# HGRN2 steps that make their own weight pairs on ScalarE and VectorE, in a two-layer encoder trunk

## The chip, the core and the metric

The kernel runs on one core of one Trainium2 chip. The metric is the device time of one execution in microseconds (us). Five engines work side by side, each with its own queue that runs in order: TensorE (PE; its weight loads are PEld), VectorE (DVE), ScalarE (ACT), GpSimd (POOL) and SyncE (SP, which here only issues transfers).

## The reference, cut to what matters

Layer 0 is a sparse attention beside a gMLP gate, layer 1 is an HGRN2 recurrence; each is followed by a ConvFFN. D = 1024, T = 1024, f32.

```python
def hgrn2(q, f, i, lb):                      # 8 heads, chunks of 64
    q = silu(q); g = lb + (1 - lb) * sigmoid(f)
    k = 1.0 - g; log_g = log(g)
    def step(S, (qb, kb, ib, lgb)):
        b = cumsum(lgb, axis=-2)
        inter = (qb * exp(b)) @ S
        a = einsum('td,tsd,sd->ts', qb, where(causal, exp(b_t - b_s), 0), kb)
        S_new = exp(b_last)[..., None] * S + (kb * exp(b_last - b)).T @ ib
        return S_new, inter + a @ ib
...
# layer 1: q, f, i, gate = split_cols(h @ c_w_in); o = rms_norm(hgrn2(...), c_out_norm)
#          y = (o * silu(gate)) @ c_w_out
# layer 0: dsa_attention: top-256 keys of an indexer's score per query, then softmax(q k + bias) v over those
```

## The kernel before, in words

Every large product is taken with a high and a low f32r part of both operands: three matmuls (lines 107 to 109, `mm3`). So each block of weights (128x1024 f32, tile `raw`, two buffers) is turned into a pair `whi`, `wlo` (four buffers each). `weights` does it on POOL: a copy that rounds (line 76) and a subtraction (line 77). `split` (lines 111 to 113) does the same on ACT and DVE; it serves activations.

The attention of layer 0 (pools `at`, `at2`) runs 48 steps: eight heads, six steps each over the query blocks (0,1), (2,3), 4, 5, 6, 7. At step t PE makes the logits of step t (`probabilities`), turns the probabilities of step t-2 (`transposed`), and for odd heads multiplies the values of step t-3 (`values`, line 595) for that head and the even one before it. So the values of a pair of heads lie in six steps in a row, and the next six have none. PE's order is the written one here (`manual_schedule`); the other engines are ordered by a planner from its own costs. Before it stand the top-256 search on DVE (lines 492 to 528) and the projections; `v_t` takes its last columns by four ACT copies (line 477).

The HGRN2 layer is 64 steps: eight groups (two halves of the sequence by four pairs of heads), and in each group eight steps p = 0 to 7, four chunks of 128 for two heads. PE, DVE and ACT keep the written order in the whole loop; POOL and SP follow the planner. A step s, in order of writing:

- `exponents` of step s+2: four matmuls into `ep`, two ACT exponentials (line 870) into `ex`; `operands` of s+2: nine DVE instructions (lines 879 to 887).
- a piece of the next group's projections, one of two kinds by p: `forget`, `query`, `value`, or this group's `gate`. Its 24 or 48 matmuls (lines 107 to 109) are most of PE's step. `forget` ends in a sigmoid and three DVE instructions (lines 824 to 826: gates and key).
- `output` of step s: three products into `ok`, a tile of `bank` (two buffers), where `at` is an operand (line 968); ACT copies the result, DVE updates the state from it (line 975).
- `levels` of step s+1: products into `lv` (line 939), and from them `at`: a DVE product with the identity (944), three DVE masked copies, three ACT block copies (951), two more DVE masked copies (954).

Once per group and half of it: `logs` (Ln, its high part on ACT, its low part `ll` on POOL, line 832) at p = 2; `key_turn` at the end of p = 3, 4 (with two POOL products for `gq`, lines 846 and 847); and for the group before: `squares` and `sums` at p = 0, 1, `spread` (two diagonal tiles `dg` on DVE, line 913) at p = 3, 4, `broadcast` (PE, line 919, into a tile of `bank`) at the start of p = 4, 5 and `finish` (DVE, 923 and 924) after it. In the last group p = 2 to 7 hold `out_chunk`, columns of the output projection of the first half.

Of the kernel before, what the change touches and what calls it, by code (L numbers as in the profile page):

```python
# [38 lines left out]
def trunk(ctx, tc, a, out):  # L39
# [29 lines left out]
    def weights(src, place, m=1024, on_pool=True):  # L69
# [10 lines left out]
        return hi, lo  # L80

# [325 lines left out]
    with pool_("gm2", 2) as gp2, pool_("gm", 1) as gp, pool_("bis", 2) as bp, pool_("up", 1) as up_:  # L407
# [135 lines left out]
    with tc.tile_pool(name="at", bufs=1, reuse_waits="tile") as ap1, tc.tile_pool(name="at2", bufs=2, reuse_waits="tile") as ap2:  # L543
# [30 lines left out]
        def transposed(hd, i, l):  # L574
# [23 lines left out]

        ops, yo = ops + (bias_of(0, ap1),), None
        steps = [(hd, ii) for hd in range(8) for ii in ((0, 1), (2, 3), (4,), (5,), (6,), (7,))]  # L600
        ls, pts = {}, {}
        with tc.manual_schedule(engines={mybir.EngineType.PE}):
            for t in range(len(steps) + 3):
# [9 lines left out]
                if 2 <= t < len(steps) + 2:  # L613
                    hd, ii = steps[t - 2]
                    for i in ii:
                        pts[hd, i] = transposed(hd, i, ls.pop((hd, i)))
                if t >= 3 and steps[t - 3][0] % 2:
                    hd, ii = steps[t - 3]
                    for i in ii:
# [3 lines left out]
                        if i % 4 == 3:  # L623
                            split(y[i // 4][0][:, hd // 2], y[i // 4][1][:, hd // 2], yo)
    mix0.close()
# [151 lines left out]
    class Group:  # L777


        def __init__(self, hf, hp):  # L780
            self.hf, self.hp = hf, hp
            self.qs, self.gs, self.kT, self.gq, self.kh, self.oS, self.sq2 = ([None, None] for _ in range(7))
            self.wt = {}

        def silu(self, c0, e, nm, bufs, o=None):

            wt = w_cols(wc, c0 + (2 * self.hp + e) * P)
# [15 lines left out]
        def wide(self, c0, n, o):  # L803

            if n == 0:
                self.wt[c0] = w_wide(wc, c0 + 256 * self.hp)
            for d in range(2):
                tmaj(o[:, 256 * d:256 * d + 256], self.wt[c0], h, 4 * self.hf + 2 * n + d)
            return o.rearrange("p (c n) -> p c n", c=2)

        def forget(self, n, o=None):
# [8 lines left out]
            bc = lambda r: self.lb[:, r:r + 1].to_broadcast([P, 2, 256])  # L820
            g, k = self.i_t[:, 2 * n:2 * n + 2], self.k_t[:, 2 * n:2 * n + 2]
            o = self.wide(1024, n, pbank()) if o is None else o.rearrange("p (c n) -> p c n", c=2)
# [15 lines left out]
        def key_turn(self, e):  # L838
# [91 lines left out]
    def levels(G, c, e, ex, kl, dl, q_, k_):  # L930
        at = hw.tile([P, P], FT, name="at")
        for n in (1, 0):
            lv = lv_pool.tile([P, H], FT, name="lv")
            if n:
                pe.matmul(lv[:, 3 * P:], k_, q_, start=True, stop=True)
            for l in range(4 * n, 7 if n else 4):
# [8 lines left out]
            for l in range(4 * n, 7 if n else 4):  # L945
                w, ls = LEVELS[l], slice((l - 4 * n) * P, (l - 4 * n) * P + P)
                v = lv[:, ls]
                if l < 2:

                    for b in range(0, P, 2 * w):  # L950
                        act.copy(at[b:b + w, b + w:b + 2 * w], v[b:b + w, b + w:b + 2 * w])
                else:
                    v = second(v, w) if w > 1 else v[:, 0:64].rearrange("p (b w) -> p b w", w=w)
                    dve.copy_predicated(second(at, w), lmask[:, 64 * l:64 * l + 64].rearrange("p (b w) -> p b w", w=w), v)
        return G, c, e, ex, dl, at

    def output(G, c, e, ex, dl, at):
# [19 lines left out]
    def out_chunk(m):  # L977

        wt = w_cols(a["c_w_out"][0], m * P)
# [14 lines left out]
    steps = [(g, c, e) for g in groups for c in range(4) for e in range(2)]  # L994
    G = groups[0]
    for n in range(2):
        G.forget(n, fg[n])
    G.logs()
    for n in range(2):

        G.value(n, lv_pool.tile([P, H], FT, name="lv"))
    G.query(0, ex_pool.tile([P, H], FT, name="ep"))
    with tc.manual_schedule(engines={mybir.EngineType.PE, mybir.EngineType.DVE, mybir.EngineType.Activation}):
        G.key_turn(0)
        G.key_end(0)
        ops = [G.operands(*G.exponents(0, 0)[1:])]
        G.query(1, pbank())
        G.key_turn(1)
        ats = [levels(*ops.pop(0))]
        ops.append(G.operands(*G.exponents(0, 1)[1:]))  # L1010
        for s, (G, c, e) in enumerate(steps):
# [5 lines left out]
            if g in (4, 5, 7) and p in (2, 5, 6, 7) and not (g == 5 and p > 5):  # L1017
                back = (G if g == 7 else groups[3]).fetch((2, 5, 6, 7).index(p) + (4 if g == 5 else 0))
            if p == 0:
                G.key_end(1)  # L1020
            if p in (4, 5) and L:
                L.broadcast()
            if p == 6 and N:
                N.key_end(0)
# [152 lines left out]
```

## Time and profile before

| | us |
|---|---|
| three timed runs | 2982.4, 2980.08, 2980.15 (median 2980.15) |
| profiled execution | 2982.33, of which the span from first to last instruction is 2980.5 |
| PE busy | 2835.9 (95% of the span) |
| DVE / ACT / POOL busy | 1912.8 / 867.2 / 1254.8 |
| granted PE clock, mean over the span | 0.981 |

The profile gives each instruction's start and length on its engine, and for an idle engine the instruction that ended its wait. The sequence of stages by time: projections and search to 473 us, attention to about 613, output projection and first ConvFFN to about 1465, HGRN2 to about 2190, then the second output projection and ConvFFN.

### The profile page before, as it was taken

How to read it: one execution, taken by the hardware profiler on the slowest of the kernel's cores; microseconds unless marked ns; L12 is line 12 of the kernel's file. 1: busy time of each engine (PE TensorE's matmuls, PEld its weight loads, DVE VectorE, ACT ScalarE, POOL GpSimd, SP SyncE). 2: the span in 40 equal slices, each digit the busy share in tenths (PEclk: the TensorE clock that was granted, in tenths of full speed). 3: DMA queues.
4: the chain of work that ended last, by engine and by line, in shares of the span. 5: the costliest groups of instructions: out<-in, count | busy, mean ns of one | idle time of the engine just before them, and what ended most of it. 6: DMA issues, size and time to landing. Idle time of an engine off the chain costs nothing.

```text
span 2980.5 us, 39089 instructions
## 1 busy us (share of the span) xinstructions
PE 2835.9 (95%) x15173; PEld 2403.8 (81%) x15188; DVE 1912.8 (64%) x3739; ACT 867.2 (29%) x1644; POOL 1254.8 (42%) x820
## 2 busy tenths in 40 slices
PE   7989996999999999999889999999999999999998
PEld 6779885778888888888788898888778888888887
DVE  5779998746545544545877777877665544445446
ACT  4555314622111111112343333333222111111112
POOL 3116622366433433334554444444355433434433
PEclk9999998999999999999899999999999999999999
DMA  4301222333111111112322212222252111111112
GB/s 164 94 29 40 85 85 57 86 110 117 43 57 50 50 44 49 50 43 76 105 63 64 65 54 67 65 71 68 85 166 71 50 43 43 57 50 44 49 50 78
DMA packets 243524, 204.09 MB, mean 68 GB/s; under 512 B 9137, under 2 KB 215778, under 8 KB 243338
## 3 DMA queue, kind: packets, MB, share of 16 engines
q1 hardware_dynamic: 230704, 177.68, 19.2%
q10 hardware_dynamic: 12634, 23.90, 2.6%
q8 instruction: 120, 1.97, 0.3%
q14 instruction: 66, 0.54, 0.1%
HBM read 180.01 MB, written 26.26 MB: 69 GB/s over the span
## 4 chain that ended last, share of the span: by engine, by line
PE 73%; DVE 19%; ACT 4%; POOL 2%; issue 1%; DMA 0%; ACTq 0%; POOLq 0%; SPq 0%; DVEq 0%
PE pbank L107 10%; PE pbank L108 10%; PE pbank L109 10%; DVE junk L492 6%; PE dn L107 5%; PE dn L108 5%; PE dn L109 5%; PE bank L107 5%; PE bank L109 5%; PE bank L108 5%; PE lv L939 2%; DVE cand L512 1%; DVE ex L882 1%; PE pbank L595 1%; PE twobank L363 1%
## 5 line engine op out<-in xcount | busy, mean ns | idle before, releaser
L76 POOL TENSOR_SCALAR whi<-raw 128x1024 fp32r<-128x1024 f32 x268 | 289.7, 1084 | 915.0 <-PE pbank L108 503.3
L77 POOL TENSOR_TENSOR wlo<-raw,whi 128x1024 fp32r<-128x1024 f32 x268 | 652.4, 2438 | 17.8
L107 PE MATMUL pbank<-bhi,whi 128*128 128x512 f32 (+2 forms) x1352 | 522.6, 387 | 3.3 <-DVE xt L638 3.0
L108 PE MATMUL pbank<-blo,whi 128*128 128x512 f32 (+2 forms) x1352 | 522.9, 387 | 0.0
L109 PE MATMUL pbank<-bhi,wlo 128*128 128x512 f32 (+2 forms) x1352 | 522.2, 386 | 0.0
L687 DVE TENSOR_TENSOR xt<-xt,dn 128x512 f32<-128x512 f32 x352 | 235.0, 682 | 151.5 <-PE dn L109 151.2
L654 DVE SCALAR_TENSOR_TENSOR cy<-pbank,col_cv,cy 128x511 f32<-128x511 f32 (+1 forms) x176 | 130.8, 743 | 293.7 <-ACT cy L653 293.7
L107 PEld LDWEIGHTS pbank<-bhi,whi 128*128 128x128 f32 (+1 forms) x1352 | 255.1, 189 | 55.1 <-POOL whi L76 3.8
L109 PEld LDWEIGHTS pbank<-bhi,wlo 128*128 128x128 f32 (+1 forms) x1352 | 255.1, 189 | 52.1
L108 PEld LDWEIGHTS pbank<-blo,whi 128*128 128x128 f32 (+1 forms) x1352 | 255.3, 189 | 50.3
L654 DVE SCALAR_TENSOR_TENSOR cy<-bank,col_cv,cy 128x511 f32<-128x511 f32 (+1 forms) x176 | 131.8, 749 | 241.6 <-ACT cy L653 238.7
L107 PE MATMUL dn<-ghi,whi 128*128 128x512 f32 x704 | 279.1, 397 | 0.6 <-ACT ghi L675 0.5
L108 PE MATMUL dn<-glo,whi 128*128 128x512 f32 x704 | 279.0, 396 | 0.0
L109 PE MATMUL dn<-ghi,wlo 128*128 128x512 f32 x704 | 278.5, 396 | 0.0
L107 PE MATMUL bank<-bhi,whi 128*128 128x512 f32 x704 | 274.8, 390 | 0.0
L109 PE MATMUL bank<-bhi,wlo 128*128 128x512 f32 x704 | 274.1, 389 | 0.0
L108 PE MATMUL bank<-blo,whi 128*128 128x512 f32 x704 | 273.9, 389 | 0.0
L676 POOL TENSOR_TENSOR glo<-cy,ghi 128x512 fp32r<-128x512 f32 x88 | 114.3, 1298 | 344.7 <-ACT ghi L675 344.7
L653 ACT ACTIVATE cy<-bank,col_cv,col_cv 128x512 f32<-128x512 f32 x88 | 68.1, 774 | 473.9 <-PE bank L109 473.9
L492 DVE TENSOR_SCALAR_CACHE_REDUCE junk<-tri,cand 128x1024 bf16<-128x1024 f32 (+1 forms) x186 | 175.9, 946 | 0.0
L654 DVE SCALAR_TENSOR_TENSOR cy<-halo,col_cv,cy 128x1 f32<-128x1 f32 (+1 forms) x176 | 173.8, 987 | 0.0
L107 PEld LDWEIGHTS dn<-ghi,whi 128*128 128x128 f32 x704 | 132.3, 188 | 33.4 <-DVE xt L687 1.0
(325 smaller groups left out, 5821.7 us busy)
## 6 DMA issues: line engine op xcount, KB each, us to landing
raw<-in_ffn_w_up_dram SPq DMA_DIRECT2D x96, 512.0 KB
raw<-in_c_w_in_dram SPq DMA_DIRECT2D x64, 512.0 KB
raw<-in_ffn_w_down_dram SPq DMA_DIRECT2D x48, 512.0 KB
raw<-in_ab_w_in_dram SPq DMA_DIRECT2D x28, 512.0 KB
raw<-in_ab_w_out_dram SPq DMA_DIRECT2D x16, 512.0 KB
raw<-in_c_w_out_dram SPq DMA_DIRECT2D x16, 512.0 KB
xo<-xd ACTq DMA_DIRECT2D x24, 256.0 KB
ts_d<-td ACTq DMA_DIRECT2D x8, 576.0 KB
```

The source lines that it names most:

```text
L76: pool.tensor_scalar(out=hi, in0=raw, scalar1=1.0, scalar2=1.0, op0=OP.mult, op1=OP.mult)
L77: pool.tensor_tensor(out=lo, in0=raw, in1=f(hi), op=OP.subtract)
L107: pe.matmul(o, lhs[0], rhs[0], start=start, stop=False)
L108: pe.matmul(o, lhs[0], rhs[1], start=False, stop=False)
L109: pe.matmul(o, lhs[1], rhs[0], start=False, stop=stop)
L363: pe.matmul(s[:, c0:c0 + cn], q_, ka[:, c0:c0 + cn], start=True, stop=False)
L492: dve.tensor_scalar(out=junk[:, 0:n], in0=acc[i], scalar1=cand, scalar2=None, op0=OP.is_ge, op1=OP.add, accum_out=cnt)
L653: act.activation(y, o, AF.Identity, scale=cw2[:, c:c + 1], bias=cb[:, c:c + 1])
L654: mac = lambda d, s_, w: dve.scalar_tensor_tensor(out=d, in0=s_, scalar=w[:, c:c + 1], in1=d, op0=OP.mult, op1=OP.add)
L676: pool.tensor_tensor(out=lo, in0=yb, in1=f(hi), op=OP.subtract)
L687: dve.tensor_tensor(out=xt[hf][:, m], in0=xt[hf][:, m], in1=o, op=OP.add)
L939: pe.matmul(lv[:, ls], kl[:, l], ex[:, l], start=True, stop=True)
```

## The change

In HGRN2, `raw_unit` loads the weights of one unit one step ahead; `pair_of` splits them on ACT and DVE, one unit in each of the 64 steps (`ahead` says which), one step or more before PE uses it; the first two units of group 1 are split ahead of the loop. POOL makes no pair for the groups 1 to 7 and for `out_chunk`. The low part of the logarithm and `gq` go from POOL to DVE, and the key 1 - g from DVE to ACT. The masks of `at` are made in two parts: the fine levels as before, the ACT blocks and the last two masked copies at the start of the next step. Gates, logs, key turn, spread, broadcast, finish and key end each come a step later or in smaller pieces. In the attention the values of the first three pairs of heads lie in every second step of eleven; all values stand ahead of the transposes of their step, `pt1` has nine buffers, and the instructions that the attention puts on the engine of `v_last` are queued behind it.

```diff
+    def raw_unit(src, place):
+
+        raw = wpool.tile([P, 1024], FT, name="raw", bufs=2)
+        nc.sync.dma_start(place(raw), src)
+
+        def pair_of():
+            hi, lo = (wpool.tile([P, 1024], FR, name=n, bufs=4) for n in ("whi", "wlo"))
+            split(hi, lo, raw)
+            return place(hi), place(lo)
+
+        return pair_of
...
-                act.activation(v_t[:, 4 * hf:4 * hf + 4, 256 * c:256 * c + 256], o, AF.Copy)
+                v_last = act.activation(v_t[:, 4 * hf:4 * hf + 4, 256 * c:256 * c + 256], o, AF.Copy)
...
-    with tc.tile_pool(name="at", bufs=1, reuse_waits="tile") as ap1, tc.tile_pool(name="at2", bufs=2, reuse_waits="tile") as ap2:
+    with tc.tile_pool(name="at", bufs=1, reuse_waits="tile") as ap1, tc.tile_pool(name="at2", bufs=2, reuse_waits="tile") as ap2, \
+            tc.issue_after(v_last.ins):
...
-                pt = ap2.tile([P, H], FT, name="pt1", bufs=6) if hd % 2 else all_[:, g * P:g * P + w]
+                pt = ap2.tile([P, H], FT, name="pt1", bufs=9) if hd % 2 else all_[:, g * P:g * P + w]
...
+        for t, (hd, ii) in enumerate(steps):
+            if hd % 2:
+                when[t + 3 + (t % 6 if hd < 7 else 0)] = (hd, ii)
...
-                if t >= 3 and steps[t - 3][0] % 2:
-                    hd, ii = steps[t - 3]
+                if t in when:
+                    hd, ii = when[t]
...
-            act.activation(g, o, AF.Sigmoid)
+            self.f[n] = self.wide(1024, n, pbank()) if o is None else o.rearrange("p (c n) -> p c n", c=2)
+
+        def sigmoids(self):
+
+            for n in range(2):
+                act.activation(self.i_t[:, 2 * n:2 * n + 2], self.f[n], AF.Sigmoid)
+
+        def gates(self):
+            bc = lambda r: self.lb[:, r:r + 1].to_broadcast([P, 4, 256])
+            g = self.i_t
             dve.tensor_tensor(out=g, in0=g, in1=bc(1), op=OP.mult)
             dve.tensor_tensor(out=g, in0=g, in1=bc(0), op=OP.add)
-            dve.tensor_scalar(out=k, in0=g, scalar1=-1.0, scalar2=1.0, op0=OP.mult, op1=OP.add)
 
         def logs(self):
             g = self.i_t
+            act.activation(self.k_t, g, AF.Identity, scale=-1.0, bias=ones[:, 0:1])
             act.activation(g, g, AF.Ln)
             act.activation(self.lh, g, AF.Copy)
-            pool.tensor_tensor(out=self.ll, in0=g, in1=f(self.lh), op=OP.subtract)
+
+        def low_logs(self):
+            dve.tensor_tensor(out=self.ll, in0=self.i_t, in1=f(self.lh), op=OP.subtract)
...
+        def odd_queries(self, e):
+
             q, t = self.qs[e], hw.tile([P, 256], FT, name=f"gq{e}")
-            pool.tensor_tensor(out=t, in0=odd(q), in1=odd(self.kT[e]), op=OP.mult)
-            pool.tensor_tensor(out=t, in0=odd(q), in1=t, op=OP.subtract)
+            dve.tensor_tensor(out=t, in0=odd(q), in1=odd(self.kT[e]), op=OP.mult)
+            dve.tensor_tensor(out=t, in0=odd(q), in1=t, op=OP.subtract)
...
-        wt = w_cols(a["c_w_out"][0], m * P)
+        wt = groups[7].pairs.pop(0)
...
                 x = n[0].exponents(*n[1:])
-                ops.append(n[0].operands(*x[1:]))
+
+            at, low = ats[0][-2:]
+            blocks(at, low)
+            if x:
+                ops.append(x[0].operands(*x[1:]))
+            for l in (2, 3):
+                masked(at, low, l)
+            to, pair_of = made
+            to.pairs.append(pair_of())
+            made = ahead(s + 1) if s + 1 < len(steps) else None
+            if p in (5, 6) and L:
+                L.finish(p - 5)
             if p in (4, 5) and L:
-                L.finish(p - 4)
-            if p in (3, 4) and L:
-                L.spread(p - 3)
+                L.spread(p - 4)
...
             if N:
+                if p == 2:
+                    N.gates()
+                if p == 3:
+                    N.logs()
+                if p == 4:
+                    N.low_logs()
+                if p in (5, 6):
+                    N.odd_queries(p - 5)
                 (N.forget, N.query, N.value, G.gate)[p // 2](p % 2)
+                if p == 1:
+                    N.sigmoids()
```

## Rows read from the trace of the kernel before

**Rows 1.** The page, its first part: busy us of each engine.
```profile
PE 2835.9 (95%) x15173; PEld 2403.8 (81%) x15188; DVE 1912.8 (64%) x3739; ACT 867.2 (29%) x1644; POOL 1254.8 (42%) x820
```
**Rows 2.** Busy time in stretches: ConvFFN; then HGRN2's eight groups and their sum.
```profile
core 0: us, PE busy (x) PEld busy (x) DVE busy (x) ACT busy (x) POOL busy (x), PEclk, DMA share, GB/s
...
760.00:1420.00 660.00, 659.96 (x2881) 540.00 (x2880) 330.56 (x453) 119.05 (x204) 264.39 (x164) 1.00 0.17 52
...
1510.00:1625.00 115.00, 110.19 (x773) 102.51 (x772) 84.72 (x211) 49.12 (x106) 54.35 (x34) 1.00 0.20 60
1625.00:1709.06 84.06, 77.87 (x529) 72.45 (x528) 61.20 (x155) 30.24 (x70) 37.22 (x24) 0.96 0.19 60
...
1967.10:2044.80 77.70, 75.19 (x529) 70.03 (x528) 57.77 (x145) 30.64 (x71) 36.99 (x23) 1.00 0.20 61
...
2126.40:2190.00 63.60, 53.32 (x264) 44.21 (x265) 46.63 (x93) 14.34 (x37) 24.76 (x16) 0.95 0.36 113
sum 680.00, PE 628.37 PEld 577.03 DVE 504.85 ACT 238.64 POOL 299.78; mean PE 78.55 PEld 72.13 DVE 63.11 ACT 29.83 POOL 37.47
```
**Rows 3.** Waits of PE from 1475 to 2230 us: total us, times, longest.
```profile
PE bank L919 <- DVE st L975: 22.6, 7, 4.9
PE bank L968 <- ACT ex L870: 15.2, 8, 4.1
PE bank L919 <- DVE dg L913: 7.9, 3, 3.9
...
PE bank L857 <- POOL ll L832: 2.1, 1, 2.1
```
**Rows 4.** PE in order of time, one group's turn from p = 3 to 4.
```profile
1629.89 1.22 PE L919 MATMUL bank<-dg,ones_r 128*128 128x512 f32 x2 [4.86 <-DVE st L975]
...
1632.29 0.41 PE L107 MATMUL pbank<-whi,bhi 128*128 128x256 f32 x1
```
**Rows 5.** POOL in order of time, the same turn.
```profile
1622.92 2.66 POOL L77 TENSOR_TENSOR wlo<-raw,whi 128x1024 fp32r<-128x1024 f32 x1
```
**Rows 6.** DVE in order of time, the same turn.
```profile
1614.67 0.69 DVE L882 TENSOR_TENSOR ex<-ex,q 128x512 f32<-128x512 f32 x1
...
1623.48 2.66 DVE L882 TENSOR_TENSOR ex<-ex,q 128x512 f32<-128x512 f32 x1
...
1629.49 0.34 DVE L975 SCALAR_TENSOR_TENSOR st<-st,dl,bank 128x128 f32<-128x128 f32 x1
```
**Rows 7.** Groups of DVE instructions, 1520 to 2190 us: busy us, mean ns.
```profile
L879 DVE TENSOR_TENSOR kl<-ex,kT 128x512 f32<-128x512 f32 x61 | 58.0, 951 | 31.1 <-ACT ex L870 28.9
...
L826 DVE TENSOR_SCALAR k_t<-i_t 128x512 f32<-128x512 f32 x13 | 13.9, 1066 | 0.4
...
L909 DVE CAST r4h<-r 128x4 fp32r<-128x4 f32 x16 | 4.7, 297 | 1.4 <-POOL r L172 1.4
```
**Rows 8.** DVE in order of time at the start of the attention.
```profile
473.83 1.23 DVE L399 TENSOR_TENSOR skb<-raw,ska 128x1024 fp32r<-128x1024 f32 x1
477.78 0.69 DVE L113 TENSOR_TENSOR blo<-bank,bhi 128x512 fp32r<-128x512 f32 x1 [2.72 <-ACT bhi L112]
```
**Rows 9.** Groups of ACT instructions, 1520 to 2190 us.
```profile
L823 ACT ACT_TABLE_LOAD x13 | 16.7, 1283 | 0.2
...
L831 ACT ACTIVATE lh<-i_t 128x1024 fp32r<-128x1024 f32 x7 | 7.4, 1062 | 0.2
```
**Rows 10.** ACT in order of time at the start of the attention.
```profile
464.56 1.06 ACT L392 ACTIVATE sq<-raw 128x1024 fp32r<-128x1024 f32 x1 [29.12 <-DVE e L527]
```
**Rows 11.** PE in order of time at the start of the attention.
```profile
473.25 0.58 PE L559 MATMUL twobank<-ska,sq 128*128 128x256 f32 x1 [14.09 <-ACT v_t L477]
```
**Rows 12.** Busy time in the two halves of a pair of heads, columns of rows 2.
```profile
508.11:525.70 17.59, 17.39 (x191) 14.40 (x195) 12.40 (x31) 11.00 (x24) 5.02 (x7) 1.00 0.33 92
525.70:543.32 17.62, 14.32 (x97) 10.33 (x99) 13.31 (x37) 12.30 (x28) 7.76 (x9) 1.00 0.33 91
```
**Rows 13.** SP in order of time, 608 to 625 us: loads of weights.
```profile
617.05 7.85 SPq L72 DMA_DIRECT2D raw<-in_ab_w_out_dram  x3
```
**Rows 14.** POOL in order of time, 580 to 640 us: the copy behind them.
```profile
621.01 1.04 POOL L76 TENSOR_SCALAR whi<-raw 128x1024 fp32r<-128x1024 f32 x1 [0.57 <-DMA raw<-in_ab_w_out_dram]
```

More of the change, by code (lines that the diff above doesn't have):

```diff
@@ L624, in trunk @@
                             split(y[i // 4][0][:, hd // 2], y[i // 4][1][:, hd // 2], yo)
+                if 2 <= t < len(steps) + 2:
+                    hd, ii = steps[t - 2]
+                    for i in ii:
+                        pts[hd, i] = transposed(hd, i, ls.pop((hd, i)))
     mix0.close()
@@ L805, in wide @@
             if n == 0:
-                self.wt[c0] = w_wide(wc, c0 + 256 * self.hp)
+                if self.pairs:
+                    self.wt = [(hi[:, k], lo[:, k]) for hi, lo in (self.pairs.pop(0), self.pairs.pop(0)) for k in range(4)]
+                else:
+                    self.wt = w_wide(wc, c0 + 256 * self.hp)
             for d in range(2):
-                tmaj(o[:, 256 * d:256 * d + 256], self.wt[c0], h, 4 * self.hf + 2 * n + d)
+                tmaj(o[:, 256 * d:256 * d + 256], self.wt, h, 4 * self.hf + 2 * n + d)
             return o.rearrange("p (c n) -> p c n", c=2)
@@ L935, in levels @@
                 pe.matmul(lv[:, 3 * P:], k_, q_, start=True, stop=True)
+            else:
+                low = lv
             for l in range(4 * n, 7 if n else 4):
@@ L944, in levels, with masked, blocks, output @@
                 dve.tensor_tensor(out=at, in0=lv[:, 3 * P:], in1=ident, op=OP.mult)
[L945 to L957, printed above, removed]
+                for l in range(4, 7):
+                    masked(at, lv, l)
+        return G, c, e, ex, dl, at, low
+    def masked(at, lv, l):
+        w, ls = LEVELS[l], slice(l % 4 * P, l % 4 * P + P)
+        v = second(lv[:, ls], w) if w > 1 else lv[:, ls][:, 0:64].rearrange("p (b w) -> p b w", w=w)
+        dve.copy_predicated(second(at, w), lmask[:, 64 * l:64 * l + 64].rearrange("p (b w) -> p b w", w=w), v)
+    def blocks(at, lv):
+        for l in range(2):
+            w, v = LEVELS[l], lv[:, l * P:l * P + P]
+            for b in range(0, P, 2 * w):
+                act.copy(at[b:b + w, b + w:b + 2 * w], v[b:b + w, b + w:b + 2 * w])
+    def output(G, c, e, ex, dl, at, low):
         hd, ce, cc = 2 * G.hp + e, slice(P * e, P * e + P), slice(c * P, c * P + P)
@@ L994, in trunk, with ahead @@
     steps = [(g, c, e) for g in groups for c in range(4) for e in range(2)]
+    def ahead(s):
+        g, p = s // 8, s % 8
+        if g == 7:
+            to, u = groups[7], (a["c_w_out"][0].rearrange("(k p) c -> p k c", p=P)[:, :, p * P:p * P + P],
+                                lambda r: r.rearrange("p (k c) -> p k c", c=P))
+        elif p < 4:
+            to, u = groups[g + 1], groups[g + 1].units()[2 + p]
+        elif p < 6:
+            to, u = groups[g], groups[g].units()[2 + p]
+        elif g < 6:
+            to, u = groups[g + 2], groups[g + 2].units()[p - 6]
+        else:
+            to, u = groups[7], groups[7].units()[p]
+        return to, raw_unit(*u)
     G = groups[0]
@@ L997, in trunk @@
         G.forget(n, fg[n])
+    G.sigmoids()
+    G.gates()
     G.logs()
+    G.low_logs()
     for n in range(2):
@@ L1002, in trunk @@
     G.query(0, ex_pool.tile([P, H], FT, name="ep"))
+    for u in groups[1].units()[0:2]:
+        groups[1].pairs.append(raw_unit(*u)())
     with tc.manual_schedule(engines={mybir.EngineType.PE, mybir.EngineType.DVE, mybir.EngineType.Activation}):
         G.key_turn(0)
+        G.odd_queries(0)
         G.key_end(0)
@@ L1007, in trunk @@
         G.query(1, pbank())
+        made = ahead(0)
         G.key_turn(1)
+        G.odd_queries(1)
         ats = [levels(*ops.pop(0))]
@@ L1053, in trunk @@
                 L.sums(p)
-            if p in (3, 4) and N:
-                N.key_turn(p - 3)
+            if p in (4, 5) and N:
+                N.key_turn(p - 4)
         G.squares(0)
```

34 lines of the change are left out of this document (17 added, 17 removed).

## The prediction

> **What bounds the kernel now.** I read the page first, then busy time by stretch, then the waits of PE, then single turns in order of time. PE is busy 95% of the span, and no other engine over 64% [rows 1]. The stretches say where the other 5% lies. In the ConvFFN nothing of it: 659.96 of 660 us at full clock, and the change touches nothing there. In HGRN2 the eight groups take 680 us with PE busy in 628.37 of them, and in some of them the mean granted clock falls to 0.95 or 0.96 [rows 2]. One group there runs at clock 1.00 throughout, and PE is busy in 75.19 us of it, while the one from 1625 takes 84.06 us. 75.2 us is what PE needs for a group; the rest is waiting and its aftermath.
>
> The waits name two places [rows 3]: the broadcast (line 919) for a DVE state update or for the diagonal tiles, 30.5 us together, and the product with `at` (line 968), 15.2 us. One turn shows both costs. PE stands still for 4.86 us before the broadcast, and 2.4 us after it a 256-column matmul takes 0.41 us where 0.28 is usual: PE runs at 1.2 GHz, the lower of its two levels, after the pause [rows 4]. The mean clock of 0.96 over the 84.06 us around it [rows 2] is a loss of 3.4 us, so such a gap costs its own length and some three microseconds more.
>
> Why is DVE late? In the same turn POOL makes the low half of a weight pair from 1622.92 for 2.66 us [rows 5], and the DVE product issued in that time takes 2.66 us, while the same instruction took 0.69 us at 1614.67 [rows 6]. DVE stands still while POOL reads two operands. By line, the means are 951 ns where 690 is the free length, 1066 where 427 is, 297 where 160 is (free lengths being those of most instances) [rows 7]. I took the excess over the free length for each of 13 such groups from 1520 to 2190 us, and they sum to about 100 us, some 12.5 us in a group. The state update that frees the broadcast's bank stands behind this in DVE's queue (1629.49) [rows 6].
>
> **The change, part by part.**
>
> *Pairs to ACT and DVE.* Each step gets an ACT copy of 128x1024, 1.06 us as `lh` [rows 9], and a DVE subtraction of that size, 1.23 us [rows 8]. For eight steps: ACT +8.5 us, DVE +9.8. With `low_logs` (1.23 us), `gq` (four 256-column products, between 0.35, half of a 512 one's 0.69, and 0.69; I take 0.42 each, 1.7) and the key taken away (two at 0.43, 0.9), DVE gets +11.9 us a group (the gates' four products become two of twice the length), and loses about 12.5 us of standing still. So DVE stays at some 61 us of the 75.2 that PE needs. ACT goes from 30.2 us [rows 2] to about 37: the pairs, the key's 1.06 us, and two table loads less of 1.28 us [rows 9], since both sigmoids now stand together. Neither is full. What changes is the form: eight even portions of 1.23 us at fixed places in place of blocks of 2.4 us that fall on any instruction.
>
> The Trainium skill speaks against this. Its page Perfetto Trace Analysis, section Optimizing Scalar/DVE Operations, says that moving work between GpSimd and VectorE might not help, since they share a port to SBUF. By the totals just given it would be right (11.9 against 12.5 us a group), and the time would be that of my third rival. I weigh it below the place of the work, which it doesn't speak of.
>
> *Masks in two parts, gates at later steps.* Before, ACT waited for `at` copies that stood behind the masks and then held the next exponentials; now the exponentials go first and the ACT blocks after them. The three DVE instructions of the gates stood in each `forget` step ahead of the state update; now two larger ones stand in p = 2 alone, after the masks. The longest chain of ACT is at p = 3: pair, key, Ln and high part at 1.06 each and two table loads at 1.28 [rows 9], 6.8 us; the rest of ACT's work was at most 30.2/8 = 3.8 us a step on average. So the step holds 6.8 to 10.6 us against a PE step of 75.2/8 = 9.4, and may run over by a microsecond once a group. Behind it are that step's state update, the next masks and the operands of p = 4.
>
> *Spread and broadcast a step later.* They move together, so DVE has the same distance as before. The bank that the broadcast takes at p = 5 is the one that the state update of p = 4 frees, and ahead of that update now stand the pair (1.23) and `low_logs` (1.23). So this wait need not vanish. It lies between 0 and the 4.86 us of before. The nearest row is the group at clock 1.00: 77.70 us with 75.19 busy [rows 2], 2.5 us of waits, with POOL's blocking still in it. That group stayed at full clock with them. I take 2.0 us a group, without a loss of clock.
>
> *Loads of weights.* SP issues each load a step ahead of its split. At the end of the attention a load issued from 617.05 on was there for POOL at 621.01, after a wait of 0.57 us [rows 13, 14]: at most 4.0 us, against a lead of 9.4. Costed at nothing, under the rest of that step; without that cover each microsecond would count 64 times, once a step. SP's queue also carries the stores and fetches of `yd` and `xd`; these wait for DVE results of the same step and would hold the load behind them by part of a step only.
>
> *Start of HGRN2.* PE waited 2.1 us for `ll` behind three pairs in POOL's queue [rows 3]; on DVE it follows `lh` at once. But two pairs of group 1 are new there (2.5 us of DVE, 2.1 of ACT). Between -2 and +5 us; I take 2 gained.
>
> *Values spread.* The two halves of a pair of heads last the same, 17.6 us, but PE is busy 17.39 us in the one with most values and 14.32 in the other [rows 12], where it waits at the transposes for the chain of DVE, ACT and POOL. Values put there fill at most 3.3 us for each of three pairs, 9.9 in all; the half that loses them then waits on that chain itself, so at the least nothing comes of it. I take half, 5 us.
>
> *Queued behind `v_last`.* ACT stands 29.12 us, to 464.56, before an attention operand that waits for DVE, with two `v_t` copies behind it [rows 10]; PE's first attention matmul waits 14.09 us for these [rows 11]. But the mask work on DVE ends there too, so only what DVE then idles is won: 2.72 us ahead of the first splits [rows 8] and some tenths in the next ones. 0 to 6 us; I take 3.
>
> *The sum*, against the profiled execution (2982.33 us, its span 2980.5 and 1.8 around it). Six middle groups: 680 - 115 - 63.6 = 501.4 us, less 6 x 75.2 = 451.2, is 50.2, of which 12 stay: 38. First group: 115 - 110.19 = 4.8 idle, 3 won. Last: 10.3 idle and about 3 of low clock, but its `out_chunk` steps keep their chain of DVE and ACT: 6. Start 2. HGRN2 together 49, attention 5 + 3 = 8. That is 57 us: 2925.3. The profiled run stands 2.2 us above the median of the timed runs (0.07%), so for the median I say 2923 us.
>
> **The rivals.**
>
> *The wait moves along.* DVE is at the broadcast of p = 5 as late as it was at p = 4, for `low_logs` and ACT's long p = 3 lie ahead of it. For it: it's the same bank and the same distance. Against it: 2 us of blocking in just that turn are gone [rows 6]. Price: 3 to 4.9 us in each of six groups and 2.5 of low clock each, 33 to 44 us, less the 12 already kept: 2944 to 2955.
>
> *Slower.* ACT and DVE now meet the weights in the written order. Should a load land after its split's turn, the split holds the state update and the masks behind it, and PE stands. Price: the lateness, in each of 64 steps, so the 57 us are gone at 0.9 us late each, which is a landing 10.3 us after issue. From there it is slower: at 11 us, 1.6 x 64 = 102 us against 57, about 3025. The 4.0 us speak against it [rows 14].
>
> *Nothing comes of it.* DVE's total stays and PE waits as often elsewhere; attention brings nothing: 2975 to 2985. That is the outcome that the page cited above would lead one to. Against it: the waits sit at fixed turns, and these are taken apart.
>
> *More than forecast.* All waits go and attention fills: 50 + 5 + 13 + 2 + 10 + 6 = 86 us, below 2900.
>
> **How the numbers follow.** Forecast (2900 to 2940) 0.62, the wait moves (2940 to 2965) 0.24, nothing 0.05, slower 0.05, below 2900 0.04. What a measurement tells from no change here is about 0.2%, 6 us. Faster 0.62 + 0.24 + 0.04 = 0.90, same 0.05, slower 0.05. For the range I take the forecast and most of the first rival, 2900 to 2955, which leaves out about 0.04 below and 0.15 above; the forecast's own range is 2900 to 2940.
>
> **What would show it.** Right: POOL nearly idle in HGRN2; DVE products of 512 columns at 0.69 us throughout; groups of 76 to 78 us at clock 0.99 or 1.00; the waits at lines 919 and 968 under 15 us together; first attention matmul before 473 us or DVE's first splits without the gap. Wrong: a wait of several microseconds at the broadcast of p = 5 with the lower clock after it (first rival); ACT or DVE waiting for `raw` (second); DVE's instructions as long as before with POOL idle, which would mean that I misread who holds whom.

## The result, and the profile after

The changed kernel takes 2925.47 us (median of four runs, 2924.47 to 2929.79), the one before, on the same chip, 2980.11: a ratio of 0.9819, 95% interval 0.9802 to 0.9836. Its profiled execution took 2925.3 us, with a span of 2923.5. The forecast was 2923 us for the median and 2925.3 for the profiled execution; the prediction was right, and so were most of its terms. Some of its reasons were not, as the experiments show.

The page's first part, busy us of each engine, answers to [rows 1]:

```profile
PE 2822.3 (97%) x15172; PEld 2390.0 (82%) x15188; DVE 1893.0 (65%) x3813; ACT 922.5 (32%) x1704; POOL 971.5 (33%) x648
```

PE is busy 13.6 us less for the same matmuls: that part of the gain isn't waiting but clock, as the stretches below show. Where the 57 us came from shows best between points that exist in both kernels. I take the output's product with `at` at the start of groups two, eight, and of the last step, and the end of HGRN2. Busy time in these stretches, first of before, then of after (columns of [rows 2]; the first stretch of each is six groups):

```profile
1592.63:2096.33 503.70, 465.74 (x3148) 431.87 (x3147) 378.00 (x926) 183.81 (x428) 224.56 (x139) 0.97 0.21 64
2096.33:2168.49 72.16, 65.51 (x362) 56.48 (x361) 49.55 (x124) 16.69 (x51) 27.29 (x18) 0.95 0.30 95
2168.49:2227.78 59.29, 54.13 (x248) 44.09 (x248) 41.62 (x54) 13.13 (x22) 36.45 (x22) 1.00 0.54 173
```

```profile
1578.31:2041.56 463.25, 451.83 (x3148) 419.04 (x3147) 357.10 (x980) 223.40 (x471) 12.09 (x12) 1.00 0.23 69
2041.56:2106.46 64.90, 62.88 (x366) 54.90 (x364) 49.56 (x130) 24.56 (x59) 6.01 (x4) 1.00 0.35 113
2106.46:2170.78 64.32, 57.42 (x249) 46.61 (x248) 46.37 (x55) 13.35 (x23) 37.39 (x23) 0.95 0.54 173
```

The six groups give 40.45 us: PE's waiting falls from 503.70 - 465.74 = 38.0 to 11.4, and PE's busy time by 13.9 us, because the clock is 1.00 instead of 0.97. POOL goes from 224.56 us to 12.09. What is left there are the small powers of the output norm. DVE falls from 63.0 to 59.5 us a group although it has taken work over, ACT rises from 30.6 to 37.2.

The waits of PE, 1440 to 2190 us, answer to [rows 3]:

```profile
PE bank L959 <- DVE st L1021: 10.1, 6, 2.2
PE bank L190 <- DVE nacc L219: 4.8, 1, 4.8
PE bank L896 <- DVE gco L787: 4.7, 1, 4.7
PE bank L959 <- DVE dg L953: 4.0, 2, 3.2
...
PE bank L1014 <- DVE at L994: 1.3, 2, 1.1
```

The broadcast (now line 959) still waits for the state update, in six places, but 10.1 us in all and 2.2 at most, where it was 22.6 and 4.9, and no slower clock follows. The product with `at` (now 1014) waits 1.3 us in all. The turn of [rows 4 to 6] in the changed kernel, in order of time (DVE, ACT, PE):

```profile
1617.15 1.22 DVE L870 TENSOR_TENSOR ll<-i_t,lh 128x1024 fp32r<-128x1024 f32 x1
1618.48 0.60 ACT L874 ACTIVATE i_t<-pbank 128x512 f32<-128x512 f32 x1 [5.34 <-DVE ll L870]
1618.97 0.26 ACT L1015 COPY oS<-bank 128x128 f32<-128x128 f32 x1
1619.27 0.35 DVE L1021 SCALAR_TENSOR_TENSOR st<-st,dl,bank 128x128 f32<-128x128 f32 x1 [0.90 <-ACT oS L1015]
1619.67 0.73 PE L959 MATMUL bank<-dg,ones_r 128*128 128x512 f32 x2 [1.41 <-DVE st L1021]
```

The reader is to see a chain over two engines. ACT stands 5.34 us before it may overwrite `i_t` with the values, since `low_logs` still reads it; the output's copy stands behind that in ACT's queue, the state update behind the copy, and the broadcast's bank comes free last.

DVE's groups from 1520 to 2110 us answer to [rows 7]; then the pairs' group on ACT in the same stretch:

```profile
L125 DVE TENSOR_TENSOR wlo<-raw,whi 128x1024 fp32r<-128x1024 f32 x62 | 75.6, 1219 | 1.2 <-ACT whi L124 1.2
L922 DVE TENSOR_TENSOR ex<-ex,q 128x512 f32<-128x512 f32 x60 | 41.6, 693 | 2.1
L919 DVE TENSOR_TENSOR kl<-ex,kT 128x512 f32<-128x512 f32 x60 | 41.3, 689 | 23.6 <-ACT ex L910 23.5
```

```profile
L124 ACT ACTIVATE whi<-raw 128x1024 fp32r<-128x1024 f32 x62 | 65.8, 1061 | 1.5
```

Both products of 512 columns now have the 0.69 us that only the free ones had; for `kl` the mean was 951 ns before. And ACT stood 1.5 us in all ahead of 62 copies from `raw`: no load was late.

In the attention 7.8 us are won. I read this at a wait of 2.19 us that both kernels have ahead of HGRN2's first projection, near the end of the ConvFFN (it begins at 1435.85 and 1428.04 us; PE is busy throughout in both from 760 to 1420 us). The start of the attention in the changed kernel, PE, then DVE:

```profile
457.67 0.36 PE L572 MATMUL twobank<-ska,sq 128*128 128x256 f32 x1
...
471.31 0.29 PE L576 MATMUL twobank<-mask,bigi 128*128 128x128 bf16 x1 [13.15 <-DVE bigi L559]
```

```profile
471.03 0.22 DVE L559 TENSOR_SCALAR bigi<-ident 128x128 bf16<-128x128 f32 x1
471.28 0.69 DVE L125 TENSOR_TENSOR blo<-bank,bhi 128x512 fp32r<-128x512 f32 x1
```

The first attention product runs at 457.67 instead of 473.25 [rows 11], but PE then waits nearly as long for the masks' last work on DVE. What is won is on DVE: no gap of 2.72 us ahead of the first splits [rows 8], and mask work that ends 1.3 us sooner (its last instruction started at 472.32 before).

### The profile page after: what moved, and what is told of

It is laid out like the page before. It is cut to its first block, busy times and chain, and to the rows that moved or that the text cites. A ratio compares the mean times of both kernels' runs of the same rounds, so it can differ in the third digit from the quotient of the medians.

```text
span 2923.5 us, 38902 instructions
## 1 busy us (share of the span) xinstructions
PE 2822.3 (97%) x15172; PEld 2390.0 (82%) x15188; DVE 1893.0 (65%) x3813; ACT 922.5 (32%) x1704; POOL 971.5 (33%) x648
## 4 chain that ended last, share of the span: by engine, by line
PE 74%; DVE 18%; ACT 4%; issue 2%; POOL 1%; DMA 0%; ACTq 0%; POOLq 0%; SPq 0%; DVEq 0%
PE pbank L119 10%; PE pbank L121 10%; PE pbank L120 10%; DVE junk L504 6%; PE dn L119 6%; PE dn L120 6%; PE dn L121 6%; PE bank L119 5%; PE bank L121 5%; PE bank L120 5%; PE lv L981 2%; DVE cand L524 1%; PE twobank L375 1%; PE bank L596 1%; PE pbank L608 1%
## 5 line engine op out<-in xcount | busy, mean ns | idle before, releaser
L77 POOL TENSOR_TENSOR wlo<-raw,whi 128x1024 fp32r<-128x1024 f32 x202 | 488.4, 2423 | 12.7
L76 POOL TENSOR_SCALAR whi<-raw 128x1024 fp32r<-128x1024 f32 x202 | 215.2, 1069 | 811.8 <-PE pbank L120 387.2
L184 POOL TENSOR_TENSOR r<-r,mhalf 128x4 f32<-128x4 f32 x24 | 26.8, 1117 | 587.6 <-DVE r L183 587.6
```

The source lines that it names most:

```text
L76: pool.tensor_scalar(out=hi, in0=raw, scalar1=1.0, scalar2=1.0, op0=OP.mult, op1=OP.mult)
L77: pool.tensor_tensor(out=lo, in0=raw, in1=f(hi), op=OP.subtract)
```

## The experiments

Each is timed against the kernel before on the same chip. The table gives the median, the ratio with its interval, and the six groups as above: their time, and PE's waiting (time less busy) and clock in it, one row of busy time by stretch for each. No run is numbered e8. The kernel before has medians of 2980.1 to 2981.8 us on these chips, and the intervals reach 3 to 5 us to either side, so the medians of two changed kernels don't tell a difference of a few us. The six groups come from one profiled execution of each kernel; that of e6 took 2949.01 us, 5.3 under its median.

| kernel | median us | ratio to before | six groups us | waiting us | clock |
|---|---|---|---|---|---|
| before | 2980.11 | | 503.7 | 38.0 | 0.97 |
| after | 2925.47 | 0.9819 (0.9802 to 0.9836) | 463.3 | 11.4 | 1.00 |
| e1 pairs on POOL | 2973.16 | 0.9971 (0.9961 to 0.9982) | 501.5 | 37.1 | 0.96 |
| e2 idle POOL work | 2964.24 | 0.9941 (0.9926 to 0.9956) | 493.8 | 30.5 | 0.98 |
| e3 broadcast in pbank | 2915.15 | 0.9778 (0.9764 to 0.9793) | 452.0 | 2.1 | 1.00 |
| e4 values together | 2931.68 | 0.9832 (0.9818 to 0.9847) | | | |
| e5 not behind v_last | 2931.76 | 0.9831 (0.9815 to 0.9847) | | | |
| e6 masks together | 2954.31 | 0.9908 (0.9893 to 0.9923) | 484.3 | 25.4 | 0.98 |
| e7 broadcast earlier | 2938.82 | 0.9859 (0.9844 to 0.9874) | 474.5 | 16.5 | 0.98 |
| e9 tail and start | 2915.54 | 0.9780 (0.9766 to 0.9795) | | | |
| e10 both orders of before | 2961.89 | 0.9930 (0.9915 to 0.9945) | 492.0 | 28.1 | 0.96 |
| e11 before, with pbank | 2974.74 | 0.9979 (0.9969 to 0.9988) | 494.1 | 30.9 | 0.98 |
| e12 e3, masks together | 2941.90 | 0.9867 (0.9850 to 0.9883) | 474.3 | 14.7 | 0.99 |
| e13 logs earlier | 2964.06 | 0.9943 (0.9927 to 0.9960) | 495.0 | 29.0 | 0.96 |

**e1: the pairs back on POOL, all orders as after.**

```
 def pair_of():
     ...
-    split(hi, lo, raw)
+    pool.tensor_scalar(out=hi, in0=raw, scalar1=1.0, scalar2=1.0, op0=OP.mult, op1=OP.mult)
+    pool.tensor_tensor(out=lo, in0=raw, in1=f(hi), op=OP.subtract)
```

> The changed kernel (2925.5 us) with its 66 weight pairs of HGRN2 made on POOL again, as a copy and a subtraction there; steps, masks, gates and broadcast as changed. Theory A, POOL's two-operand work makes DVE stand still and that is most of what was lost before: DVE's 512-column products lengthen again, the broadcast waits come back, and some 25 to 45 of the 46 us won in HGRN2 are lost: 2950 to 2970 us. Theory B, the new order of the steps is what gained and it doesn't matter which engine makes the pairs: 2920 to 2932 us.

Measured 2973.16 us, just above theory A's range; theory B is out. DVE's groups (1520 to 2110 us) and PE's waits (1475 to 2230 us) in this kernel:

```profile
L920 DVE TENSOR_TENSOR kl<-ex,kT 128x512 f32<-128x512 f32 x57 | 49.4, 867 | 32.6 <-ACT ex L911 32.6
...
L954 DVE TENSOR_TENSOR dg<-ident,r4h 128x512 fp32r<-128x512 f32 x12 | 19.1, 1588 | 0.0
```

```profile
PE bank L960 <- DVE st L1022: 32.7, 9, 5.5
```

The products are long again, others than before: the diagonal tiles now stand beside POOL's work and take 1588 ns instead of after's 684. The six groups take 501.5 us of before's 503.7. So the new orders alone (with the small moves of `ll`, `gq` and the key, which e1 keeps) are worth 2 us there, and what e1 keeps is mainly the attention's 7.8.

**e2: POOL works, and nobody waits for it.** The pairs stay on ACT and DVE; POOL does two subtractions per pair into a tile that nothing reads, 2.4 us a step. This is added work; the result's computation is that of after.

```
 split(hi, lo, raw)
+for n in range(2):
+    half = f(hi)[:, n * H:n * H + H]
+    pool.tensor_tensor(out=nobody[0], in0=half, in1=half, op=OP.subtract)
```

> The changed kernel with added work on POOL that nobody waits for: after each of the 66 pairs two subtractions of 128x512 on POOL, of the pair's high part from itself, into a scratch tile. POOL's part in the data flow stays none. Theory A: the same blocking as in the run with the pairs on POOL (about 2.4 us of POOL per step): DVE gets up to 100 us longer in HGRN2 and the time goes to 2935 to 2965 us. Theory B, or a theory C in which the run with pairs on POOL is slow only because the pairs come late: 2922 to 2930 us here, with DVE's products at 0.69 us.

Measured 2964.24 us: 38.8 us for work on which nothing depends. Groups of DVE, then of POOL, 1520 to 2110 us:

```profile
L130 DVE TENSOR_TENSOR wlo<-raw,whi 128x1024 fp32r<-128x1024 f32 x58 | 89.9, 1550 | 0.4 <-issue 0.4
L931 DVE TENSOR_TENSOR dl<-dl 128x1 f32<-128x1 f32 x58 | 43.4, 748 | 2.0
...
L932 DVE TENSOR_SCALAR ex<-ex,dl 128x64 f32<-128x64 f32 x58 | 14.1, 243 | 0.0
...
L930 DVE COPY dl<-ex 128x1 f32<-128x1 f32 x58 | 8.4, 145 | 0.0
```

```profile
L94 POOL TENSOR_TENSOR nobody<-whi 128x512 f32<-128x512 f32 x116 | 136.3, 1175 | 372.8 <-ACT whi L129 368.3
```

A DVE product of one column takes 748 ns instead of 159, and the copy of one column just before it 145, as ever. One turn in order of time, POOL and DVE:

```profile
1609.26 2.44 POOL L94 TENSOR_TENSOR nobody<-whi 128x512 f32<-128x512 f32 x2 [7.25 <-ACT whi L129]
1609.51 0.15 DVE L930 COPY dl<-ex 128x1 f32<-128x1 f32 x1
1609.69 0.82 DVE L931 TENSOR_TENSOR dl<-dl 128x1 f32<-128x1 f32 x1
```

The copy, with one operand, passes beside POOL's subtraction; the product, with two, ends about when the first of the two subtractions does. The Trainium skill says this: its page SBUF — State Buffer, section Who interferes with whom, has it that a VectorE instruction with two SBUF inputs contends with a GpSimd instruction that reads SBUF, that one with at most one such input doesn't, outside the modes in which VectorE uses both of its ports, and that the one that comes second is blocked. These rows agree.

The number of operands alone doesn't decide it, though. In the kernel before, one-operand instructions are among the lengthened ones [rows 7]. The first turn below shows one of them beside a subtraction of POOL; the second, from e1, shows one beside POOL's one-operand copy (POOL, then DVE, each time):

```profile
1469.30 2.65 POOL L77 TENSOR_TENSOR wlo<-raw,whi 128x1024 fp32r<-128x1024 f32 x1
1469.68 2.56 DVE L826 TENSOR_SCALAR k_t<-i_t 128x512 f32<-128x512 f32 x1
```

```profile
1632.81 1.50 POOL L89 TENSOR_SCALAR whi<-raw 128x1024 fp32r<-128x1024 f32 x1 [14.50 <-PE pbank L122]
1633.32 1.02 DVE L950 CAST r4h<-r 128x4 fp32r<-128x4 f32 x1
```

These take 0.43 and 0.16 us in most instances. Whether they run in one of the modes that the page excepts, no run shows.

**e3: the broadcast's sum in another PSUM tile name.**

```
 def broadcast(self):
-    self.row = bank()
+    self.row = pbank()
```

> The changed kernel with the broadcast's row in a tile of pbank in place of bank, so that it doesn't wait for the state update that frees the bank. If the 1.4 to 2.2 us that PE waits there in each group are for the bank alone, they fall to the wait for the diagonal tiles, which DVE has done one subtraction of 1.23 us earlier: 7 to 10 us less, 2915 to 2919 us. If DVE is simply late there, the wait goes to the diagonal tiles or to the product with at: 2923 to 2928 us.

Measured 2915.15 us, 10.3 under after, and better than both kernels. The largest waits of PE, 1440 to 2190 us:

```profile
PE pbank L959 <- DVE dg L953: 6.7, 3, 5.2
PE bank L896 <- DVE gco L787: 4.7, 1, 4.7
```

The waits for the state update are gone; 5.2 of the 6.7 us are in the last group. The six groups take 452.0 us, 75.3 each, and PE waits 2.1 us in them: next to nothing is left to win there.

**e4 and e5: the attention's two edits undone, one each.** e4 transposes and then makes the values of the same step together; e5 takes the order behind `v_last` away.

```
-    if t in when:
-        hd, ii = when[t]
+    if 2 <= t < len(steps) + 2:
+        ...
+    if t >= 3 and steps[t - 3][0] % 2:
+        hd, ii = steps[t - 3]
     ...
-    if 2 <= t < len(steps) + 2:
-        ...
```

> The changed kernel with the attention's values back in six steps in a row, after the transposes (nine pt1 buffers and the queueing behind v_last stay). By my sum the spread is worth 5 us (0 to 10): 2930 us, with PE's waits at the transposes back to what they were. Rival: the half that lost its values waits as long as the other half gains, 2925 us.

```
 with tc.tile_pool(name="at", bufs=1, reuse_waits="tile") as ap1, \
-        tc.tile_pool(name="at2", bufs=2, reuse_waits="tile") as ap2, tc.issue_after(v_last.ins):
+        tc.tile_pool(name="at2", bufs=2, reuse_waits="tile") as ap2:
```

> The kernel after, with the attention's instructions no longer held back behind v_last on the planner's side. If the step of the sum is right (3 us, 0 to 6 possible), it takes about 2928 us, and PE stands some 29 us instead of 13.15 and a few small gaps before the first attention matmuls. Rival: the end of the mask work on DVE sets the start of the attention, whatever order ACT has; then it takes 2925 us, as the kernel after.

2931.68 and 2931.76 us. The intervals of both overlap with that of after, so I go by the traces: at the wait of 2.19 us named above e4 is 4.3 us later than after, e5 5.2; by their spans both end 5.9 us later. By this both rivals are out. In e4 PE waits 4.6 us at the transposes for POOL's `wlo` (475 to 640 us), as in before (5.4) and unlike after (0.6). In e5 the first attention product waits 14.0 us for `v_t` again, not the 29 us that I expected; the gap of 2.72 us ahead of DVE's first splits is back, and the mask work ends 2.9 us later than in after, for a reason that wasn't followed up. Together the two edits bring 7.8 us, less than the sum of what each is missed by, so they seem to overlap in part; where wasn't tried.

**e6, e7, e10: the orders of HGRN2 undone.** e6 puts each step's masks in one part: the ACT blocks and the last two masks move from the next step into `levels`, where ACT meets them before the next exponentials. e7 puts spread, broadcast and finish back to their steps of before, and the fetches with them (not shown). e10 does both.

```
 # e6
 if n:
     ...
+else:
+    blocks(at, lv)
+    for l in (2, 3):
+        masked(at, lv, l)
 ...
-at, low = ats[0][-2:]
-blocks(at, low)
 if x:
     ops.append(x[0].operands(*x[1:]))
-for l in (2, 3):
-    masked(at, low, l)
```

```
 # e7
-if p in (5, 6) and L:
+if p in (4, 5) and L:
     L.broadcast()
 ...
-if p in (5, 6) and L:
-    L.finish(p - 5)
-if p in (4, 5) and L:
-    L.spread(p - 4)
+if p in (4, 5) and L:
+    L.finish(p - 4)
+if p in (3, 4) and L:
+    L.spread(p - 3)
```

> The kernel after, with all masks of a step together again, the ACT blocks right behind the level matmuls and ahead of the next step's exponentials; pairs stay on ScalarE and VectorE. Theory A, the masks in two parts are a gain of their own: ACT stands before the blocks and holds the exponentials, the wait of the product with at for the exponentials returns (15.2 us over eight places before), 2930 to 2945 us. Theory B, that wait too came from GpSimd's lengthening of the masks, and with GpSimd silent the order of the masks is worth nothing: 2922 to 2928 us.

> The kernel after, with spread, broadcast and finish at the steps that they had before (spread at p = 3 and 4, broadcast and finish at 4 and 5) and the fetches with them. Theory A, the distance is the same and so is the time: 2922 to 2928 us, with the waits at the broadcast within 3 us of the 14.1 of the kernel after. Theory B, the long step p = 3 of ScalarE now stands right before the first broadcast: 1 to 3 us more in each of seven groups, 2932 to 2950 us.

> The kernel after with both order edits taken back together: masks of a step in one part, and spread, broadcast and finish at their old steps; pairs on ScalarE and VectorE, gates at the later steps. One by one the two cost 28.8 and 13.4 us. If each frees another wait they add up: 2968 us. If both lengthen the same wait, the one for the broadcast's bank, which no more than the 4.9 us of before and the slower clock behind it can cost in each group, the time stays at 2950 to 2960 us. If pairs on ScalarE and VectorE bring nothing without the order, 2973 us, which is before less the 8 us of the attention.

Measured 2954.31, 2938.82 and 2961.89 us. e6 is over theory A's price (2930 to 2945), but the wait didn't return where A put it, at the product with `at`. Its largest wait of ACT (1500 to 2150 us), and the turn of the broadcast, DVE and ACT and then PE:

```profile
ACT at L1005 <- DVE at L998: 143.7, 62, 4.4
```

```profile
1614.77 0.47 ACT L1005 COPY at<-lv 64x64 f32<-64x64 f32 x3 [2.03 <-DVE at L998]
1615.26 0.93 ACT L910 ACTIVATE ex<-ep 128x512 f32<-128x512 f32 x2
1615.27 0.50 DVE L998 COPY_PREDICATED at<-lmask,lv 128x64 f32<-128x64 int32 x2 [0.59 <-ACT at L1005]
1615.89 0.69 DVE L919 TENSOR_TENSOR kl<-ex,kT 128x512 f32<-128x512 f32 x1
...
1623.78 0.73 PE L959 MATMUL bank<-dg,ones_r 128*128 128x512 f32 x2 [3.56 <-DVE st L1025]
```

ACT waits for DVE's first masks in each of 62 steps (17.0 us in 17 in the kernel after), DVE for ACT's blocks, and in this turn the operands start late. All of DVE's turn up to the state update is late by it, and the gap at the broadcast is 3.56 us instead of 1.41, with the slower clock behind it (0.98 over the six groups). e7 is in theory B's range, but not by ACT's long step: DVE begins the turn ahead of the gap 33.08 us after the start of the six groups, as in after. In e7 `finish`, two products of 0.74 and 0.69 us, stands in the same step ahead of `low_logs` and the state update: the gap is 2.33 us, up to 4.31. e10 stands between the expectations: at 492.0 us the six groups lose 28.7 to after, where 21.0 and 11.2 add up to 32.2, so most of it adds; by the medians 36.4, where 28.8 and 13.4 add up to 42.2. With these two orders as they were (gates, logs and key turn stay at their later places), then, silent POOL is worth 11.7 us of the 40.45; with POOL busy the new orders are worth 2.2. The other 26.6 need both.

**e11 and e12: is the broadcast's bank the whole matter?** e11 is the kernel before with e3's edit alone, e12 is e3 with e6's.

> The kernel before, with one name changed: the broadcast's sum takes a tile of the other PSUM name (pbank), which no state update has to free. Theory A, the broadcast's bank is the one place where the late VectorE reaches TensorE: seven waits for the state update (22.6 us) and some 2.5 us of lower clock behind each go, 40 us in all, 2940 us, without any other part of the change. Theory B, VectorE stays late by GpSimd's work and TensorE waits for the next thing it owes, the diagonal tiles, the product with at or the operands: 2965 to 2980 us.

> The kernel at 2915.15 us (broadcast's sum in pbank), with the masks of a step in one part again. With the broadcast in the old tile that edit cost 28.8 us, most of it as a longer wait for the state update before the broadcast. Theory A, the late state update was the whole of it: with pbank the masks in one part cost nothing, 2913 to 2920 us. Theory B, ScalarE and VectorE waiting for each other at the masks also hold the operands and the product with at: 2925 to 2945 us.

2974.74 us and 2941.90: theory B both times. The largest waits of PE in e11 (1475 to 2230 us):

```profile
PE pbank L919 <- DVE dg L913: 22.2, 8, 3.5
PE bank L968 <- ACT ex L870: 15.2, 8, 4.1
```

The broadcast's waits of 22.6 us for the state update and 7.9 for the diagonal tiles [rows 3] became 22.2 for the diagonal tiles alone. While DVE is late, taking one of its debts off the path presents the next one: the edit brings 7.0 us (3.6 to 9.2 by the interval; 9.6 in the six groups of the profiled execution) and leaves PE 30.9 us of waiting there, not the 40 us of theory A. In the kernel after, the same edit brings about as much, 10.3 (11.3 in the six groups), but leaves 2.1 us of waiting, since nothing else is due. (For e12 the waits for the diagonal tiles are 19.2 us.)

**e9: e3, and the two longest waits left.** The last group's first diagonal tiles ahead of the seventh output chunk, and the weight pair of the first group's second query off POOL.

```
+G.pairs.append(raw_unit(*G.units()[3])())
 for u in groups[1].units()[0:2]:
 ...
+G.spread(0)
 out_chunk(6)
+G.broadcast()
 G.squares(1)
 G.sums(1)
-G.spread(0)
-G.broadcast()
```

> The broadcast's sum in the other PSUM tile name (as in the run at 2915.15 us), and two more edits: in the last group the diagonal tiles of the first head are made before the seventh output chunk instead of after it (5.2 us wait before the broadcast), and at the start of HGRN2 the weight pair of the second query goes to ScalarE and VectorE too, as one more pair in the row of two (one GpSimd pair lengthens two splits from 0.69 to 2.2 us each there, ahead of a wait of 4.7 us). If both waits go, 2906 us; if the third pair at the start costs as much as it frees, 2910; if neither moves, 2915.

2915.54 us: neither was worth anything that these runs can tell. The wait of 5.2 us at the broadcast became two, of 3.2 and 2.3; the one at line 896 fell from 4.7 to 2.5 and the end came no sooner. Why wasn't followed up.

**e13: the logs a step earlier.** This is the test of the chain that I read above.

```
 if p == 2:
     N.gates()
-if p == 3:
     N.logs()
-if p == 4:
+if p == 3:
     N.low_logs()
```

> The kernel after, with the logs (key, Ln, high part on ScalarE) at p = 2 behind the gates of the same step, and low_logs at p = 3 instead of 4; the broadcast's sum in its own tile name as in the kernel after. Theory A: the state update ahead of the broadcast of p = 5 is late because of low_logs at p = 4 (ScalarE waits some 5 us for its result before it copies the value, and the copy of the output and with it the state update stand behind that); with low_logs a step earlier the waits of 1.4 to 2.2 us at the broadcast and what they cost behind them go, 2915 us as with pbank. Theory B: ScalarE, which must now wait for the gates at p = 2, holds the next exponentials and the time is 2925 us or more, up to 2945.

2964.06 us, outside both ranges: theory A said 2915, theory B 2925 to 2945. Each has something right in its mechanism. PE's largest waits (1440 to 2190 us) and the turn of p = 2 to 3, ACT, then PE:

```profile
PE bank L1014 <- DVE at L994: 34.8, 8, 5.8
...
PE bank L959 <- DVE dg L953: 4.0, 2, 3.1
```

```profile
1607.24 1.15 ACT L865 ACTIVATE k_t<-i_t,ones 128x1024 f32<-128x1024 f32 x1 [5.12 <-DVE i_t L861]
...
1619.08 0.76 PE L1014 MATMUL bank<-at,i_t 128*128 128x128 f32 x2 [4.44 <-DVE at L994]
```

The broadcast's waits for the state update are gone, and with them ACT's wait for `ll`, as the chain said; but PE now comes to the broadcast 5.7 us later in the group, so this run alone doesn't show that the chain was the reason. What it costs is plain: ACT now stands 5.12 us for the gates of the same step, the copies and exponentials behind it come late, and the product with `at` waits 4.4 to 5.8 us in each of groups one to seven: 38.6 us lost.

## Why the prediction was right, step by step

**What bounds the kernel: right.** Late DVE turns at two places, caused by POOL's work, with a clock loss behind each gap. That DVE stands still "while POOL reads two operands" was too narrow: the cast shown under e2 is held by a one-operand copy. e1 and e2 show the cause from both sides: take POOL's silence away and 47.7 us go, or give it useless work and 38.8 go. The clock loss of about 2.5 us a gap was right as well: before has six gaps of over 3 us in the six groups (four of 4.9 at the broadcast, 3.7 and 4.1 at the product with `at`), and PE's busy time there fell by 13.9 us, 2.3 for each.

**The terms.** Six middle groups 38, measured 40.45; of the 12 us to stay, 11.4 stayed, at the very bank that was named. First group 3, measured 75.46 - 72.48 = 3.0. Start 2, measured 3.5, but elsewhere than the term said, as shown below. Attention 8, measured 7.8; the split of it (5 and 3) can't be told, as the two overlap. The last group was the mis-sized term: 6, measured 131.45 - 129.22 = 2.2. Its last steps won 7.3 us and the stretch behind them lost 5.0, with PE busy 57.42 us instead of 54.13 at clock 0.95 instead of 1.00: waits of 3.2 and 2.2 us stand there now. The sum is 57.0 us, by errors of 2.45, 1.5, -0.2 and -3.8 that cancel; that the forecast for the profiled execution is met to the tenth is luck.

**The start: the right size by luck.** Waits of PE in the start of before, 1435.85 to 1517.17 us, beside the one for `ll` [rows 3]:

```profile
PE bank L178 <- DVE nacc L207: 8.2, 1, 8.2
PE bank L856 <- ACT aft L765: 2.6, 1, 2.6
```

The wait for `ll` did fall, from 2.1 us to 0.6, but the one at the product just before it rose from 2.6 to 4.7 (now line 896), so nothing was won there. The 3.5 us come from the wait of the norm for its sum `nacc`, 8.2 us before and 4.8 after, which the prediction didn't look at. With the pairs on POOL (e1) it is 5.6; which edit shortened it the most wasn't tried.

**DVE's and ACT's totals.** DVE was to stay at 61 us a group and takes 59.5; ACT 37, measured 37.2.

**Masks in two parts: no price, and it was wrong to give none.** The step described the edit and counted it at nothing by itself. Undone alone it costs 21.0 us of the 40.45 (e6; 28.8 by the medians).

**Spread and broadcast a step later: wrong.** "DVE has the same distance as before" looked at what precedes the broadcast of its own step only. What matters is which DVE work shares the step: at the steps of before, `finish` for the first head falls ahead of the state update that the second broadcast waits for. Undone alone, 11.2 us (e7). The number came out because the residual of 2.0 us a group was taken from a row of a group that already ran well, not from this reasoning; to that extent it was luck.

**Gates and logs at later steps: right in the place, not in the weight.** p = 3 as ACT's longest step carries its load. The logs a step earlier, behind the gates of the same step, cost 38.6 us (e13). The gates' own place wasn't tried alone.

**Loads: right, with more cover than stated.** A load is issued when the split two steps earlier frees its buffer, so the lead is nearly two steps, not one. ACT's 62 copies from `raw` waited 1.5 us together.

**The rivals.** "The wait moves along" was the serious one. Its price, 2944 to 2955 us, is where e6 ends (2954.31), with the waits at the bank that it named. Its mechanism is real; with the masks in two parts there was just slack enough. "Nothing comes of it" rested on the page Perfetto Trace Analysis of the Trainium skill, section Optimizing Scalar/DVE Operations. The page says that such a move might not help; here it helped: DVE's busy time fell by 20.9 us in six groups as POOL's work moved to it and ACT.

**The signs.** Four came as named: POOL at 2.0 us a group, products of 512 columns at 0.69 us, the clock at 1.00 in the six groups, the first attention product at 457.67. Two just missed: one group of the six took 78.5 us, where 76 to 78 were named, and the waits at the two lines are 16.1 us together (10.1, 4.0 and 0.7 at the broadcast, 1.3 at the product with `at`), not under 15.

## What to carry to other kernels

When an engine is late at a fixed turn, look first for another that lengthens its instructions; a useless copy of that other work prices it. Then price each reordering with the other edits in place and without: here the silence alone gave 11.7 us, the orders alone 2.2, both together 40.45. And don't price a wait by its own length while its engine is late: in the kernel before, another PSUM tile for the broadcast brought 7 us of the 40 that its waits and the clock behind them seemed to be worth, for the next wait took its place. In the kernel after, where nothing else was due, it left PE almost nothing to wait for.

## What the runs showed of the hardware

POOL's subtraction of 128x512 holds up even a DVE product of a single column: 748 ns on the mean instead of 159 (e2). One-operand instructions can pass: a copy of one column keeps its 145 ns there. Others are held: a cast of four columns took 1.02 us instead of 0.16 beside POOL's one-operand copy (e1), a one-operand instruction of 128x512 2.56 us instead of 0.43 beside POOL's subtraction (before). And gaps differ in what follows them: after 1.41 us at the broadcast the group ran at clock 1.00 (76.72 us with PE busy 75.23), with gaps of 4.4 to 5.1 us in e13 the six groups had 0.96 and PE was busy 465.97 us instead of 451.83 for the same matmuls, 2.4 us more a gap.
